# Padding the chunks of split activations and the slots of split weights by 32 bytes, with a smaller descriptor ring

## The chip, the cores and the metric

The kernel runs on one core of a Trainium2 chip. The metric is the device time of one execution in microseconds (us). Each partition of the on-chip memory (SBUF) is a row of bytes; "byte 25184" below means the same place in all 128 partitions.

## The reference

Two transformer blocks run one behind the other on 256 tokens of width 1024, all in float32. The parts that matter here are their matrix products:

```python
def first_block(x, p, ...):
    f = swiglu(rms_norm(h, ffn1_pre_g), ffn1_w_gate, ffn1_w_up, ffn1_w_down)   # 1024 -> 2816 -> 1024
    h = h + 0.5 * rms_norm(f, ffn1_post_g)
    m = hybrid_mixer(rms_norm(h, mix_pre_g), w_in, ..., w_br_attn, w_br_pool, w_out)
    h = h + rms_norm(m, mix_post_g)
    ...                                                                       # a second swiglu
    e = (p @ ple_w_proj) * sigmoid(rms_norm(h, ple_pre_g) @ ple_w_gate)
    return h + rms_norm(e, ple_post_g)

def second_block(x, mem, ...):
    ...                                           # projections, causal attention, a convolution, two gates
    x = x + merged @ w_mix_out
    x = x + memory_cross_attention(rms_norm(x), rms_norm(mem), w_mem_q, w_mem_kv, w_mem_o)
    x = x + (silu(gate) * up) @ w_ffn_out
    return rms_norm(x, norm_final)
```

## The kernel before

All weights come from DRAM as one stream `ws` of 345 units. A unit is 512 KB, eight tiles of 128x128, and lies as 4096 bytes in each partition. SyncE loads units into five `raw` buffers (line 63). ScalarE copies a unit, rounded to the shorter float32r format, into a slot of `wh` (line 90; seven slots), and VectorE writes the rest, `raw - wh`, into a slot of `wl` (line 101; six slots). `Stream.take` hands out the eight tiles of a slot one after another, 512 bytes apart.

Activations are split in the same way. The class `Split` holds them: one tile has chunks of 128 channels, and a chunk is 1024 bytes of high part (256 tokens) and then 1024 bytes of low part. So chunk k begins 2048 k bytes behind chunk 0. `x` (eight chunks), `a` (22 chunks, inside the feed-forward layers), `o`, `y`, `m`, `mo`, `p` and `x2` are such tiles.

A product of a weight tile and a chunk takes the terms high by high, low by high and high by low. There are two forms, and the words below are used from here on:

- a **group of three** (`mm3`): three matmuls of 256 columns, `wh` on x high, `wl` on x high, `wh` on x low.
- a **pair** (`mm2`): one matmul of 512 columns (`wh` on high and low, which lie side by side) and one of 256 columns (`wl` on high). The feed-forward layers use it for most of their work.

In `mm3t` the roles are changed: the activations are the weights of TensorE and four tiles of a `wh` or `wl` slot (512 columns) are streamed past them. It is used for the values in `first_group`, with `x`, and in `mem_v_task`, with `m` and 256 columns.

Every matmul brings a weight load of 128x128 (PEld in the profile) which overlaps the matmul ahead of it. Every matmul is issued from line 197, whichever helper calls it. The order on each engine is the order in which the program is written; nothing is scheduled later.

Where the tiles lie follows from their sizes in the order of their making. `x` begins at byte 25184, `a` at 141536, `m` at 212960, `y` of the first mixer at 187616, the first slot of `wh` at 72512 and of `wl` at 101184. Divided by 128, every split activation leaves 96 and every weight slot 64.

GpSimd issues 36 small DMAs by itself; their descriptors stand in a ring that takes the first 16384 bytes of each partition. Thirteen times it also raises a sum of squares to the power -1/2 (line 286), on which a stage's scaling waits. `load_kv` (line 1118) fetches keys and values of the memory attention with eight of these DMAs.

Of the kernel before, what the change touches and what calls it, by code (L numbers as in the profile page):

```python
# [11 lines left out]
F32R = mybir.dt.float32r  # L12
# [3 lines left out]
P = 128  # L16
T = 256
D = 1024
DC = D // P
FF = 2816  # L20
FC = FF // P
# [5 lines left out]
UB = 8  # L27
LA = 4
RAW_BUFS = 5
HL_BUFS = 6  # L30
NUNITS = 345
WARM = 3
START = {0: (2, 2, 4), 1: (4, 4), 2: (4, 4), 3: (4, 4), 4: (4, 4)}

GAINS = ["ffn1_pre_g", "ffn1_post_g", "mix_pre_g", "mix_post_g", "ffn2_pre_g", "ffn2_post_g",
# [14 lines left out]
class Stream:  # L50
# [20 lines left out]
    def split_now(self, u, cuts=(UB,)):  # L71

        assert self.nhigh == self.nlow == u
        h = self.hl.tile([P, UB * P], F32R, tag="wh", name="wh", bufs=HL_BUFS + 1)
        l = self.hl.tile([P, UB * P], F32R, tag="wl", name="wl")
        r = self.R.pop(u)
        for s in self.parts(cuts):
            self.nc.scalar.copy(out=h[:, s], in_=r[:, s])  # L78
            self.nc.vector.tensor_tensor(out=l[:, s], in0=r[:, s], in1=h[:, s].bitcast(F32), op=ALU.subtract)  # L79
        self.H[u], self.L[u] = h, l  # L80
        self.nhigh = self.nlow = u + 1
# [4 lines left out]
    def split(self, u):  # L86
        while self.nhigh <= min(u + 1, NUNITS - 1):
            self.load(self.nhigh + RAW_BUFS - 2)
            h = self.hl.tile([P, UB * P], F32R, tag="wh", name="wh", bufs=HL_BUFS + 1)
            self.nc.scalar.copy(out=h, in_=self.R[self.nhigh])  # L90
            self.H[self.nhigh] = h
            self.nhigh += 1
            if self.nlow < self.nhigh - 1:
                self.low()
        while self.nlow <= min(u, NUNITS - 1):
            self.low()

    def low(self):
        u = self.nlow
        l = self.hl.tile([P, UB * P], F32R, tag="wl", name="wl")  # L100
        self.nc.vector.tensor_tensor(out=l, in0=self.R.pop(u), in1=self.H[u].bitcast(F32), op=ALU.subtract)  # L101
        self.L[u] = l
        self.nlow += 1
# [23 lines left out]
class Split:  # L127


    def __init__(self, t):  # L130
        self.t = t

    def __getitem__(self, i):
        return self.t[:, :, i]
# [5 lines left out]
class Net:  # L140
# [89 lines left out]
    def setup(self):  # L230
        nc, b, d = self.nc, self.base, self.d
        hg = b.tile([P, G_ALL + DC * T], F32, name="hg")
        self.gv, self.h = hg[:, 0:G_ALL], hg[:, G_ALL:].rearrange("p (c t) -> p c t", c=DC)
        self.x = Split(b.tile([P, DC, 2, T], F32R, name="x"))
        self.fg = b.tile([P, DC, T], F32, name="fg")
        self.ident = b.tile([P, P], F32, name="ident")
        self.ones = b.tile([P, 1], F32, name="ones")
        self.mhalf = b.tile([P, 2], F32, name="mhalf")
        self.half = b.tile([P, 4 * DC], F32, name="half")
        nc.scalar.preload_act_table_set("silu_and_others")  # L240
        at = [(0, 1), (1, 1), (2, 2), (4, 2), (6, 2)]
        for u, (lo, n) in enumerate(at):
            s = slice(G_ALL + lo * T if lo else 0, G_ALL + (lo + n) * T)
            nc.sync.dma_start(out=hg[:, s], in_=d["gx"][:, s])
            self.ws.load(u, START.get(u, (UB,)))
        nc.gpsimd.memset(self.ones, 1.0)
        nc.gpsimd.memset(self.mhalf, -0.5)
        idle = self.fg[:, 0]
        nc.vector.memset(idle, 0.0)
        w = self.abank()  # L250
        for _ in range(WARM):
            nc.tensor.matmul(w.t[:, 0:T], idle[:, 0:P], idle, start=True, stop=True)
        nc.gpsimd.dma_start(out=self.ident, in_=d["cst"][:, C_ID:C_ID + P])
        self.identr = b.tile([P, P], F32R, name="identr")
        self.after(1, lambda: nc.vector.tensor_copy(out=self.identr, in_=self.ident))
# [174 lines left out]
    def ffn(self, gate, up, down, on_chunk, nk=4):  # L430
        nc = self.nc
        x = self.x
        with self.tc.tile_pool(name="ffn", bufs=1, reuse_waits="tile") as fp:
            self.fp = fp
            a = Split(fp.tile([P, FC, 2, T], F32R, name="a"))
            aH, aL = a[0], a[1]

            def zt():
                return fp.tile([P, 2, T], F32, tag="z", name="z", bufs=6)

            def join2(z, b):
                nc.scalar.copy(out=z, in_=b.t[:, 1])  # L442
                nc.vector.tensor_tensor(out=z, in0=b.t[:, 0], in1=z, op=ALU.add)  # L443

            def evac(m, z, src):
                nc.vector.tensor_tensor(out=z, in0=src, in1=self.row(rs), op=ALU.mult)  # L446
                nc.scalar.activation(out=z[:, 0], in_=z[:, 0], func=AF.Silu)  # L447

                def s1():
                    nc.vector.tensor_tensor(out=z[:, 0], in0=z[:, 0], in1=z[:, 1], op=ALU.mult)  # L450

                def s2():
                    nc.scalar.copy(out=aH[:, m], in_=z[:, 0])

                def s3():
                    nc.vector.tensor_tensor(out=aL[:, m], in0=z[:, 0], in1=aH[:, m].bitcast(F32), op=ALU.subtract)

                self.after(1, s1)
                self.after(2, s2)
                self.after(3, s3)  # L460

            bs = [self.bank() for _ in range(nk)]
            for k in range(DC):
                for m in range(nk):
                    for sub, (name, off) in enumerate((gate, up)):
                        w = self.ws.take(name, k, off + m)
                        self.mm3(bs[m], bs[m].t[:, sub], w, x.at(k), stop=k == DC - 1)
                if k == DC - 2:
                    r = self.stat([self.acc])
                self.tick()  # L470
            rs = self.bcast_sb(r)
            for m in range(nk):
                evac(m, zt(), bs[m].t)
            for m in range(nk, FC):
                z = zt()
                for sub, (name, off) in enumerate((gate, up)):
                    b = self.bank()
                    self.wide(b, name, off + m, range(DC), x)
                    join2(z[:, sub], b)
                    if sub == 1:  # L480
                        evac(m, z, z)
                    self.tick()
            for c in range(DC):
                b = self.bank()
                two = c < DC - 1
                for k in range(FC):
                    w = self.ws.take(down, k, c)
                    if two:
                        self.mm2(b, w, a.at(k), stop=k == FC - 1)
                    else:  # L490
                        self.mm3(b, b.t[:, 0], w, a.at(k), stop=k == FC - 1)
                    if k % 8 == 4:
                        self.tick()
                on_chunk(c, b.t[:, 0], b.t[:, 1] if two else None)
# [185 lines left out]
    def mixer1(self, fills):  # L680
        nc, tc, d = self.nc, self.tc, self.d
        with tc.tile_pool(name="mix1", bufs=1, reuse_waits="tile") as mp:
# [6 lines left out]
            cnt = mp.tile([P, 4, 2, 8], F32, name="cnt")  # L689
            nc.gpsimd.dma_start(out=cnt.rearrange("p a e t -> p (a e t)"), in_=d["cst"][:, C_CNT:C_CNT + 64])  # L690
            tg2 = mp.tile([P, 4, 2, T], F32, name="tg2")
            o = Split(mp.tile([P, 4, 2, T], F32R, name="o"))
            y = Split(mp.tile([P, 4, 2, T], F32R, name="y"))
            oH, oL, yH, yL = o[0], o[1], y[0], y[1]
            tg1 = self.fg.rearrange("p (a b) t -> p a b t", b=2)

# [237 lines left out]
    def mixer2(self, x2):  # L934
        nc, tc, d = self.nc, self.tc, self.d
        W = T + P
        with tc.tile_pool(name="mix2", bufs=1, reuse_waits="tile") as mp:
# [2 lines left out]
            vz = mp.tile([P, 2, 4, 2, P], F32, name="vz")  # L940
            cv = mp.tile([P, 4, T], F32, name="cv")
            tg2 = mp.tile([P, 4, 2, T], F32, name="tg2")
            o = Split(mp.tile([P, 4, 2, T], F32R, name="o"))
            y = Split(mp.tile([P, 4, 2, T], F32R, name="y"))
            oH, oL, yH, yL = o[0], o[1], y[0], y[1]
            cs = mp.tile([P, 2, T], F32, tag="ct", name="ct", bufs=3).rearrange("p a t -> p (a t)")[:, 0:3 * P]
            tg1 = self.fg.rearrange("p (a b) t -> p a b t", b=2)
# [154 lines left out]
    def memory(self, x2):  # L1102
        nc, tc, d = self.nc, self.tc, self.d
        with tc.tile_pool(name="mem", bufs=1, reuse_waits="tile") as mp:
# [1 line left out]
            kH, kL = kx[0], kx[1]  # L1106
            vH = mp.tile([P, 2, D], F32R, name="mvH")
            vL = mp.tile([P, 2, D], F32R, name="mvL")
            o = Split(mp.tile([P, DC, 2, T], F32R, name="mo"))
            oH, oL = o[0], o[1]  # L1110

            def split(t, h, l):
# [73 lines left out]

            def trans(h):
                b = self.transposed(st[h])
                p = Split(mp.tile([P, 2, 2, T], F32R, tag="p", name="p", bufs=2))
                pH, pL = p[0], p[1]  # L1190
                bt = b.t.rearrange("p (a t) -> p a t", a=2)
                nc.scalar.copy(out=pH, in_=bt)
# [97 lines left out]
    def run(self):  # L1290
# [11 lines left out]
        self.vd = self.dram.tile([P, 2, D], F32, name="vd")  # L1302
        memctx = ExitStack()
        mpool = memctx.enter_context(tc.tile_pool(name="memx", bufs=1, side="right"))
        self.m = Split(mpool.tile([P, DC, 2, T], F32R, name="m"))
        self.mH, self.mL = self.m[0], self.m[1]
        for c in range(DC):
            self.after(14 + 3 * c, lambda c=c: self.mem_prep_chunk(c))
# [14 lines left out]
        gp2 = self.halved(1, "ffn2_post_g", 0.5)  # L1323
        plectx = ExitStack()
        self.plep = plectx.enter_context(tc.tile_pool(name="plep", bufs=1, side="right"))
        self.p = Split(self.plep.tile([P, 2, 2, T], F32R, name="p"))
        self.pH, self.pL = self.p[0], self.p[1]

        def prep_p():
# [15 lines left out]
        memctx.close()  # L1345
        self.dump("h4")
        with tc.tile_pool(name="x2p", bufs=1, side="right", reuse_waits="tile") as xp2:
            x2 = Split(xp2.tile([P, DC, 2, T], F32R, name="x2"))
            self.mixer2(x2)
            self.dump("h5")  # L1350
            self.memory(x2)
# [100 lines left out]
```

## Time and profile before

| | us |
|---|---|
| median of 2 runs | 1035.32 (1035.19 to 1035.44) |
| profiled execution, device time | 1035.02 |
| its span, first to last instruction | 1032.9 |
| PE busy | 1023.2 |
| DVE busy | 758.4 |
| ACT busy | 585.2 |
| POOL busy | 44.0 |

The device time is 2.1 us longer than the span, for what lies around it. PE is TensorE, DVE VectorE, ACT ScalarE, POOL GpSimd and SP SyncE. Matmuls are pipelined: the duration of one (its column "mean ns") is longer than the step from its start to the start of the next, and it is the steps that add up to the span. The timeline view gives starts to 0.01 us, and joins equal neighbours in one row with their count.

### The profile page before, as it was taken

Reading aid. Unit: us, or ns where it says so; the run is one execution under the profiler, and the core shown is the slowest. Engines: PE = TensorE matmul, PEld = TensorE weight load, DVE = VectorE, ACT = ScalarE, POOL = GpSimd, SP = SyncE. Lnnn points to the kernel's source line nnn. Section 1 sums busy time; section 2 is a strip of 40 time slices with the busy share of each in tenths; the row PEclk is TensorE's granted clock in tenths of the full one; section 3 lists DMA queues with packets and bytes.
Section 4 is the critical chain, followed back from the end, with each engine's and each line's share of the span. In section 5 each row is a group of like instructions: output and inputs, shape, how many; then the busy total and the mean of one; then the engine's idle time right before and its main releaser. Section 6 shows DMA issues by size and latency. Waiting matters only on the chain.

```text
span 1032.9 us, 18212 instructions
## 1 busy us (share of the span) xinstructions
PE 1023.2 (99%) x7280; PEld 961.8 (93%) x7280; DVE 758.4 (73%) x1191; ACT 585.2 (57%) x979; POOL 44.0 (4%) x73
## 2 busy tenths in 40 slices
PE   9999999999999999999999999999999999999997
PEld 8988888999999998888899999999999999888886
DVE  7798865687868678888457776886678767878652
ACT  7567655464644556655456565464556555656531
POOL 0000000120000110000000111000001000000000
PEclk9999999999999999999999999999999999999999
DMA  8676665555545755666645666554566345766541
GB/s 292 221 217 193 204 212 175 194 191 183 195 143 168 230 181 174 194 201 185 204 170 178 201 199 199 156 176 151 163 218 232 106 136 198 216 186 185 183 161 42
DMA packets 55013, 191.34 MB, mean 185 GB/s; under 512 B 6400, under 2 KB 7936, under 8 KB 54928
## 3 DMA queue, kind: packets, MB, share of 16 engines
q1 hardware_dynamic: 52992, 184.37, 55.2%
q0 software_dynamic: 1936, 5.80, 1.9%
q8 instruction: 57, 0.93, 0.4%
q14 instruction: 28, 0.23, 0.1%
HBM read 187.00 MB, written 3.15 MB: 184 GB/s over the span
## 4 chain that ended last, share of the span: by engine, by line
PE 81%; issue 16%; DMA 1%; DVE 1%; SPq 0%; POOL 0%; POOLq 0%; DVEq 0%; ACT 0%
PE mm L197 77%; PE at L197 3%; DMA raw<-ws 1%; PE at L876 1%; DMA hg<-gx 0%; DVE sqp L337 0%; POOL r L286 0%; DVE wl L79 0%; SPq L63 0%; DVE wl L101 0%; DVE x L312 0%; DVE fg L1363 0%; POOLq L1445 0%; DVEq L1445 0%; ACT wh L78 0%
## 5 line engine op out<-in xcount | busy, mean ns | idle before, releaser
L197 PE MATMUL mm<-x,wh 128*128 128x256 f32 (+1 forms) x2784 | 650.3, 315 | 0.1
L197 PE MATMUL mm<-x,wl 128*128 128x256 f32 x1824 | 512.3, 281 | 0.9 <-DVE wl L101 0.4
L197 PEld LDWEIGHTS mm<-x,wh 128*128 128x128 f32 x2784 | 459.5, 188 | 35.5 <-ACT wh L78 1.0
L101 DVE TENSOR_TENSOR wl<-raw,wh 128x1024 fp32r<-128x1024 f32 x340 | 409.1, 1218 | 11.4 <-ACT wh L90 5.2
L90 ACT CAST wh<-raw 128x1024 fp32r<-128x1024 f32 x340 | 349.3, 1046 | 39.5 <-PE mm L197 30.3
L197 PEld LDWEIGHTS mm<-x,wl 128*128 128x128 f32 x1824 | 343.8, 189 | 2.7 <-DVE wl L79 1.2
L197 PE MATMUL mm<-a,wh 128*128 128x512 f32 (+1 forms) x594 | 185.2, 368 | 0.0
L197 PE MATMUL mm<-a,wl 128*128 128x256 f32 x528 | 147.5, 280 | 0.0
L197 PEld LDWEIGHTS mm<-a,wh 128*128 128x128 f32 x594 | 107.2, 188 | 19.1
L197 PEld LDWEIGHTS mm<-a,wl 128*128 128x128 f32 x528 | 99.2, 188 | 0.0
L447 ACT ACTIVATE z<-z 128x256 f32<-128x256 f32 x66 | 27.2, 418 | 80.5 <-DVE z L446 80.5
L443 DVE TENSOR_TENSOR z<-mm,z 128x256 f32<-128x256 f32 x108 | 45.3, 420 | 30.0 <-ACT z L442 29.8
L442 ACT COPY z<-mm 128x256 f32<-128x256 f32 x108 | 39.5, 366 | 33.0 <-PE mm L197 32.7
L308 ACT ACTIVATE x<-hg 128x256 fp32r<-128x256 f32 x56 | 27.5, 537 | 42.3 <-DVE hg L381 22.1
L286 POOL TENSOR_TENSOR r<-v,mhalf 128x2 f32<-128x2 f32 x13 | 17.6, 1354 | 677.6 <-DVE v L284 677.6
L446 DVE TENSOR_TENSOR z<-z,rs 128x512 f32<-128x512 f32 x54 | 37.4, 692 | 1.8
L353 DVE TENSOR_TENSOR fg<-mm,fg 128x256 f32<-128x256 f32 x14 | 5.9, 425 | 40.7 <-ACT fg L352 40.7
L450 DVE TENSOR_TENSOR z<-z 128x256 f32<-128x256 f32 x66 | 27.2, 424 | 8.1 <-ACT z L447 2.7
L312 DVE SCALAR_TENSOR_TENSOR x<-hg,x 128x256 fp32r<-128x256 f32 x56 | 26.8, 514 | 6.8 <-ACT x L308 6.8
L352 ACT COPY fg<-mm 128x256 f32<-128x256 f32 x14 | 5.2, 373 | 42.0 <-PE mm L197 42.0
L327 DVE TENSOR_TENSOR acc<-acc,sq 128x256 f32<-128x256 f32 x27 | 11.5, 425 | 23.6 <-ACT sq L326 23.5
L197 PE MATMUL mm<-y,wh 128*128 128x256 f32 x136 | 27.8, 283 | 0.0
(217 smaller groups left out, 1033.6 us busy)
## 6 DMA issues: line engine op xcount, KB each, us to landing
raw<-ws SPq DMA_DIRECT2D x340, 512.0 KB, 4.1
raw<-ws SPq DMA_DIRECT2D x9, 256.0 KB, 5.8
ub<-ub SPq DMA_DIRECT2D x8, 160.0 KB, 2.8
mraw<-memT POOLq DMA_DIRECT2D x8, 128.0 KB, 4.2
kd<-kv POOLq DMA_DIRECT2D x8, 128.0 KB, 3.3
vd<-kv POOLq DMA_DIRECT2D x4, 256.0 KB, 4.3
kv<-kd POOLq DMA_DIRECT2D x4, 256.0 KB, 5.9
kv<-vd POOLq DMA_DIRECT2D x4, 256.0 KB, 6.7
```

The lines of the kernel that those rows point to most:

```text
L90: self.nc.scalar.copy(out=h, in_=self.R[self.nhigh])
L101: self.nc.vector.tensor_tensor(out=l, in0=self.R.pop(u), in1=self.H[u].bitcast(F32), op=ALU.subtract)
L197: self.nc.tensor.matmul(out, lhsT, rhs, start=not b.started, stop=stop, skip_group_check=True)
L286: nc.gpsimd.tensor_tensor(out=r, in0=v, in1=self.mhalf, op=ALU.pow)
L308: self.nc.scalar.activation(out=self.ordered(x[0][:, c]), in_=self.rows(self.h[:, c]), func=AF.Copy, scale=gain(c))
L312: self.nc.vector.scalar_tensor_tensor(out=l, in0=self.rows(self.h[:, c]), scalar=gain(c), in1=h, op0=ALU.mult, op1=ALU.subtract)
L327: nc.vector.tensor_tensor(out=acc, in0=acc, in1=s, op=ALU.add)
L442: nc.scalar.copy(out=z, in_=b.t[:, 1])
L443: nc.vector.tensor_tensor(out=z, in0=b.t[:, 0], in1=z, op=ALU.add)
L446: nc.vector.tensor_tensor(out=z, in0=src, in1=self.row(rs), op=ALU.mult)
L447: nc.scalar.activation(out=z[:, 0], in_=z[:, 0], func=AF.Silu)
L450: nc.vector.tensor_tensor(out=z[:, 0], in0=z[:, 0], in1=z[:, 1], op=ALU.mult)
```

## The change

Each chunk of a split activation gets 8 more float32 (32 bytes) behind its low part, so that chunk k begins 2080 k bytes behind chunk 0. Each slot of `wh` and `wl` gets 32 bytes as well, so that slots lie 4128 bytes apart; the tiles inside a slot stay 512 bytes apart. `raw` is not changed. GpSimd's ring is cut from 16384 to 8192 bytes in each partition, and the room takes the padding. No instruction is added, removed, moved or given another shape; the order on every engine is the same.

After it, `x` begins at byte 16992, `a` at 134016, the first slot of `wh` at 64576 and of `wl` at 93472. Divided by 128, the chunks of an activation leave 96, 0, 32, 64, 96 and so on for k = 0, 1, 2, 3, 4 (for `a` and those behind it the row begins at another place), and the slots of `wh` leave 64, 96, 0, 32 and so on.

```diff
+SKEW = 8
...
+    def high(self):
+        return self.hl.tile([P, UB * P + SKEW], F32R, tag="wh", name="wh", bufs=HL_BUFS + 1)[:, 0:UB * P]
+
+    def low_tile(self):
+        return self.hl.tile([P, UB * P + SKEW], F32R, tag="wl", name="wl")[:, 0:UB * P]
...
     def __init__(self, t):
-        self.t = t
+        self.t = t[:, :, 0:2 * T].rearrange("p n (i t) -> p n i t", i=2)
...
-        self.x = Split(b.tile([P, DC, 2, T], F32R, name="x"))
+        self.x = Split(b.tile([P, DC, 2 * T + SKEW], F32R, name="x"))
...
-            a = Split(fp.tile([P, FC, 2, T], F32R, name="a"))
+            a = Split(fp.tile([P, FC, 2 * T + SKEW], F32R, name="a"))
...
-    nc = bacc.Bacc("TRN2", target_bir_lowering=False, num_devices=1)
+    nc = bacc.Bacc("TRN2", target_bir_lowering=False, num_devices=1, dynamic_dma_scratch_size=8192)
```

The tiles `o`, `y`, `mo`, `p`, `m` and `x2` are changed as `x` and `a` are.

## Rows read from the trace of the kernel before

**Rows 1.** The page: span, busy time of each engine, granted clock.

```profile
span 1032.9 us, 18212 instructions
...
PE 1023.2 (99%) x7280; PEld 961.8 (93%) x7280; DVE 758.4 (73%) x1191; ACT 585.2 (57%) x979; POOL 44.0 (4%) x73
...
PEclk9999999999999999999999999999999999999999
```

**Rows 2.** Groups of instructions of PE, each shape apart.

```profile
L197 PE MATMUL mm<-x,wl 128*128 128x256 f32 x1824 | 512.3, 281 | 0.9 <-DVE wl L101 0.4 <-DVE wl L79 0.4
L197 PE MATMUL mm<-x,wh 128*128 128x256 f32 x1920 | 350.1, 281 | 0.1
L197 PE MATMUL mm<-x,wh 128*128 128x512 f32 x864 | 300.2, 391 | 0.0
L197 PE MATMUL mm<-a,wh 128*128 128x512 f32 x462 | 161.1, 393 | 0.0
```

**Rows 3.** The chain that ended last, in order of time: start us, us, what.

```profile
30.37 83.22 PE mm L197 x480
```

**Rows 4.** Timeline of PE, first feed-forward layer: pairs (start us, us).

```profile
60.03 0.39 PE L197 MATMUL mm<-x,wh 128*128 128x512 f32 x1
60.26 0.28 PE L197 MATMUL mm<-x,wl 128*128 128x256 f32 x1
60.38 0.39 PE L197 MATMUL mm<-x,wh 128*128 128x512 f32 x1
```

**Rows 5.** Timeline of PE, merge of the first mixer: groups of three.

```profile
314.90 0.28 PE L197 MATMUL mm<-y,wl 128*128 128x256 f32 x1
...
315.26 0.28 PE L197 MATMUL mm<-y,wl 128*128 128x256 f32 x1
...
315.62 0.28 PE L197 MATMUL mm<-y,wl 128*128 128x256 f32 x1
```

**Rows 6.** Timeline of PE, output product of the first mixer; three groups between these rows.

```profile
339.79 0.28 PE L197 MATMUL mm<-x,wl 128*128 128x256 f32 x1
...
341.19 0.28 PE L197 MATMUL mm<-x,wl 128*128 128x256 f32 x1
```

**Rows 7.** Timeline of PE, the same product of the second mixer, as many groups.

```profile
764.84 0.28 PE L197 MATMUL mm<-x,wl 128*128 128x256 f32 x1
...
766.25 0.28 PE L197 MATMUL mm<-x,wl 128*128 128x256 f32 x1
```

**Rows 8.** Timeline of PE, `mem_v_task`: weight slots streamed past `m`, as many groups.

```profile
590.80 0.28 PE L197 MATMUL mm<-wl,m 128*128 128x256 f32 x1
...
592.24 0.28 PE L197 MATMUL mm<-wl,m 128*128 128x256 f32 x1
```

**Rows 9.** Timeline of PE, `first_group` of the second mixer: six matmuls of 512 columns.

```profile
612.92 0.39 PE L197 MATMUL mm<-wh,x 128*128 128x512 f32 x1
613.15 0.40 PE L197 MATMUL mm<-wl,x 128*128 128x512 f32 x1
613.38 0.63 PE L197 MATMUL mm<-wh,x 128*128 128x512 f32 x2
...
614.32 0.28 PE L197 MATMUL mm<-x,wh 128*128 128x256 f32 x1
```

**Rows 10.** DMA view of 750 to 800 us: busy tenths in 40 slices.

```profile
DMA  7557167988999960573814838039019999689997
```

**Rows 11.** Timeline of POOL, the loads of `load_kv` and the power between them.

```profile
756.70 1.12 POOL L1118 DMA_DIRECT2D kv<-kd  x2 [101.11 <-PE mm L197]
757.81 0.73 POOL L1118 DMA_DIRECT2D kv<-vd  x1
758.53 0.56 POOL L1118 DMA_DIRECT2D kv<-kd  x1
...
789.61 1.11 POOL L286 TENSOR_TENSOR r<-v,mhalf 128x2 f32<-128x2 f32 x1 [1.01 <-DVE v L284]
```

**Rows 12.** Line 1118 in the trace: time from issue to landing.

```profile
DMA to landing us min/median/max: 5.1/6.2/7.8
```

More of the change, by code (lines that the diff above doesn't have):

```diff
@@ L73, in split_now @@
         assert self.nhigh == self.nlow == u
-        h = self.hl.tile([P, UB * P], F32R, tag="wh", name="wh", bufs=HL_BUFS + 1)
-        l = self.hl.tile([P, UB * P], F32R, tag="wl", name="wl")
+        h, l = self.high(), self.low_tile()
         r = self.R.pop(u)
@@ L88, in split @@
             self.load(self.nhigh + RAW_BUFS - 2)
-            h = self.hl.tile([P, UB * P], F32R, tag="wh", name="wh", bufs=HL_BUFS + 1)
+            h = self.high()
             self.nc.scalar.copy(out=h, in_=self.R[self.nhigh])
@@ L96, in split @@
             self.low()
+    def high(self):
+        return self.hl.tile([P, UB * P + SKEW], F32R, tag="wh", name="wh", bufs=HL_BUFS + 1)[:, 0:UB * P]
+    def low_tile(self):
+        return self.hl.tile([P, UB * P + SKEW], F32R, tag="wl", name="wl")[:, 0:UB * P]
     def low(self):
         u = self.nlow
-        l = self.hl.tile([P, UB * P], F32R, tag="wl", name="wl")
+        l = self.low_tile()
         self.nc.vector.tensor_tensor(out=l, in0=self.R.pop(u), in1=self.H[u].bitcast(F32), op=ALU.subtract)
@@ L691, in mixer1 @@
             tg2 = mp.tile([P, 4, 2, T], F32, name="tg2")
-            o = Split(mp.tile([P, 4, 2, T], F32R, name="o"))
-            y = Split(mp.tile([P, 4, 2, T], F32R, name="y"))
+            o = Split(mp.tile([P, 4, 2 * T + SKEW], F32R, name="o"))
+            y = Split(mp.tile([P, 4, 2 * T + SKEW], F32R, name="y"))
             oH, oL, yH, yL = o[0], o[1], y[0], y[1]
@@ L942, in mixer2 @@
             tg2 = mp.tile([P, 4, 2, T], F32, name="tg2")
-            o = Split(mp.tile([P, 4, 2, T], F32R, name="o"))
-            y = Split(mp.tile([P, 4, 2, T], F32R, name="y"))
+            o = Split(mp.tile([P, 4, 2 * T + SKEW], F32R, name="o"))
+            y = Split(mp.tile([P, 4, 2 * T + SKEW], F32R, name="y"))
             oH, oL, yH, yL = o[0], o[1], y[0], y[1]
@@ L1108, in memory @@
             vL = mp.tile([P, 2, D], F32R, name="mvL")
-            o = Split(mp.tile([P, DC, 2, T], F32R, name="mo"))
+            o = Split(mp.tile([P, DC, 2 * T + SKEW], F32R, name="mo"))
             oH, oL = o[0], o[1]
@@ L1188, in trans @@
                 b = self.transposed(st[h])
-                p = Split(mp.tile([P, 2, 2, T], F32R, tag="p", name="p", bufs=2))
+                p = Split(mp.tile([P, 2, 2 * T + SKEW], F32R, tag="p", name="p", bufs=2))
                 pH, pL = p[0], p[1]
@@ L1304, in run @@
         mpool = memctx.enter_context(tc.tile_pool(name="memx", bufs=1, side="right"))
-        self.m = Split(mpool.tile([P, DC, 2, T], F32R, name="m"))
+        self.m = Split(mpool.tile([P, DC, 2 * T + SKEW], F32R, name="m"))
         self.mH, self.mL = self.m[0], self.m[1]
@@ L1325, in run @@
         self.plep = plectx.enter_context(tc.tile_pool(name="plep", bufs=1, side="right"))
-        self.p = Split(self.plep.tile([P, 2, 2, T], F32R, name="p"))
+        self.p = Split(self.plep.tile([P, 2, 2 * T + SKEW], F32R, name="p"))
         self.pH, self.pL = self.p[0], self.p[1]
@@ L1347, in run @@
         with tc.tile_pool(name="x2p", bufs=1, side="right", reuse_waits="tile") as xp2:
-            x2 = Split(xp2.tile([P, DC, 2, T], F32R, name="x2"))
+            x2 = Split(xp2.tile([P, DC, 2 * T + SKEW], F32R, name="x2"))
             self.mixer2(x2)
```

## The prediction

> **What bounds the kernel now.** I read the page first. [...] So nothing that ends a wait earlier can help much: about 10 us of the span are not PE's. A change pays, or costs, through the step from one matmul to the next.
>
> The groups by shape [rows 2] say how much there is of what. There are 864 + 462 = 1326 matmuls of 512 columns on `x` and `a`, so 1326 pairs. Of 7280 matmuls that leaves 7280 - 2 x 1326 = 4628, nearly all of 256 columns in groups of three, so about 1500 groups.
>
> The chain and the timeline give the steps, since durations of pipelined matmuls overlap. The chain has a stretch of 480 matmuls, 240 pairs, in 83.22 us [rows 3]: 346.7 ns a pair. Inside a pair the 512 columns take 0.23 us and the 256 columns 0.12 [rows 4]; the mean over the 240 pairs of that stretch, of starts that the view rounds, is 228.3 and 118.3 ns. So a pair takes 0.3467 us and 1326 of them 460 us. The remaining 573 us are mostly groups of three. These do not all cost the same: 0.36 us in the first mixer's merge [rows 5]; (341.19 - 339.79) / 4 = 0.350 in its output product [rows 6]; 1.41 / 4 = 0.3525 in the second mixer's output product [rows 7].
>
> Two things in this matter here. First, the 256 columns that a matmul of 512 has more than one of 256 take 228.3 - 118.3 = 110 ns. A matmul of 256 columns takes 116.7 (0.350 / 3) to 120, so some 7 to 10 ns of each step are not streaming; in a pair it is 8.3. This is all that any placement of data could give back. Second, [rows 6] and [rows 7] are the same code on the same tile `x` with the same tiles inside slots, and differ by 2.5 ns a group, 0.7%, with no change of place at all.
>
> **The change part by part.** No instruction is added, taken away or reshaped, so there is no work to count. What changes is where a streamed chunk lies against the weight tile that is loaded under it. That is a price per matmul, times some 7000.
>
> Does the place matter? Before, the remainders by 128 of all streamed activations (96) and all weight slots (64) are fixed, so their distance is always 32. Beyond this, distances by 512 differ between tiles: 288 for `x`, 416 for `a`, `y` and `o`. Pairs on `x` and on `a` show no difference that I can find in their groups (mean duration 391 and 393 ns) [rows 2]. For the groups of three, tiles at 416 take 0.36 us [rows 5] and the tile at 288 takes 0.350 or 0.3525 [rows 6, 7]. That could be the place, or the rhythm in which PE happens to run: the 2.5 ns between rows 6 and 7 are rhythm alone.
>
> The other distances stand in the trace where the roles are changed. With a slot streamed past `m` (distance 96 by 128) the four groups take 1.44 us, 0.360 each [rows 8]. With a slot streamed past `x` (96 as well) six matmuls of 512 columns take 614.32 - 612.92 = 1.40 us, 233.3 ns each [rows 9], where a pair's 512 columns take 228.3 (346.7 less 118.3, the 256 columns). So what there is of another distance is 5 ns dearer per 512 columns, and at the dear end for 256. This speaks for a small loss, not for a gain; but these rows have another operand in each role, so it is no proof.
>
> The row on the first cause that comes to mind, other traffic, is against it: between 757 and 777 us the DMA engines go from idle to full and back [rows 10] and the groups keep their 0.3525 us [rows 7]. So the lost 8.3 ns lie between PE's own two streams or inside PE.
>
> [...]
>
> For the sum I take this: pairs stay at 346.7 ns, since both tiles that use them have that step. Groups of three lose today's rhythm, because distances now change from chunk to chunk, and get a mean of the three steps seen, (350 + 352.5 + 360) / 3 = 354.2 ns. Today's mean I estimate at 351.5, as 1920 / 2 = 960 of the 1500 groups are on `x` [rows 2]. So 1500 x 2.7 ns = 4.0 us more. The bounds lie 8.3 ns a matmul below (7000 x 8.3 = 58 us) and, above, at the dearest steps seen: per pair 233.3 - 228.3 = 5.0 and 120 - 118.3 = 1.7, so 1326 x 6.7 = 8.9 us, and per group 360 - 351.5 = 8.5, so 1500 x 8.5 = 12.8 us; together 21.7 us.
>
> The other engines are bystanders. DVE and ACT read and write the padded tiles along the partition as before; they are busy 73% and 57% of the span [rows 1], and a per cent on their instructions would stay under PE. If that cover were gone, PE would wait for `wl`, which it now does for 0.9 us in all [rows 2].
>
> The ring: GpSimd issues four loads in 756.70 to 759.09, of 256 KB each, with no gap between them [rows 11], while each takes 5.1 to 7.8 us to land [rows 12]. So four were in flight in 16 KB of ring. If half the ring held only two, the third would wait up to 6 us; behind it on POOL's queue stand the fourth load and, 31 us later, the power at 789.61. Both have that slack, so I cost it at nothing.
>
> Against its own time the profiled execution becomes 1035.0 + 4.0 = 1039.0; it is 0.3 us under the median of 1035.3, which makes 1039.3. I forecast 1039.
>
> **The rivals.** *Other distances are dearer (slower).* One mechanism: PE's weight load and its stream disturb each other, least at the distance of 32 that all tiles now have. After the change three quarters of the matmuls have another one. Price: 0.75 x 21.7 = 16 us, 1051; if the quarter that stands nowhere in the trace (64) is worse than these, more. It passes 2% (20.7 us) from 3.0 ns a matmul on the mean of 7000. For it: [rows 8, 9]. Against it: the changed roles, and that `a` and `x` agree.
>
> *The padding breaks a collision (faster).* The 8.3 ns are then a collision that comes of everything being a power of two apart, and distances that move from chunk to chunk avoid it in half of the cases: 0.5 x 58 = 29 us, 1006. For it: the loss is the same on nearly every matmul, as a fixed alignment would make it. Against it: the distances 288, 416 (by 512) and those of [rows 8, 9] all have it. [...]
>
> *The ring bites.* POOL's loads wait for ring space one by one, and the power that scales the queries comes late. Price: at most about 8 us, the longest landing, so 1043. Against it: the 31 us between these loads and the power [rows 11].
>
> **How the numbers follow.** Forecast (no price beyond rhythm, 1031 to 1045): 0.55. Dearer distances: 0.28, about half of it beyond 2%. Collision broken: 0.14, most of it beyond 2%. Ring: 0.03. So faster by over 2% (under 1014.6; about what a measurement of this kernel can tell from no change) 0.12, slower by over 2% (above 1056) 0.15, and the rest, 0.73, within. The range reaches from the collision rival's middle (1008) to somewhat over the dear rows (1058).
>
> **What the profile will show.** If I am right, pairs on `x` step by 346 to 348 ns and groups of three by 350 to 357, with the DVE and ACT rows unchanged. Pairs above 350 mean the dearer distances; pairs under 340 mean the collision. A step that changes with chunk k inside one product would show that distance itself has the price. I am wrong if 64, the distance that no row shows, is far from the others, or if the remainder of the streamed chunk counts by itself: 0 and 32 by 128 are new as well.

## The result, and the profile after

The changed kernel takes 1042.71 us (1042.06 to 1043.36, 2 runs), 1.0074 of the kernel before, interval 1.0057 to 1.0091. So it is slower by 7.4 us, inside the range on record and 3.7 us above the forecast of 1039.0. The profiled execution took 1042.06 us for a span of 1039.9.

The page of the changed kernel, as in [rows 1]:

```profile
span 1039.9 us, 18204 instructions
...
PE 1030.8 (99%) x7280; PEld 964.5 (93%) x7280; DVE 758.3 (73%) x1191; ACT 584.9 (56%) x979; POOL 44.0 (4%) x73
...
PEclk9999999999999999999999999999999999999999
```

PE does the same 7280 matmuls at the same granted clock (a mean of 0.998 of full speed in both) and is busy 7.6 us longer; DVE, ACT and POOL did not move. The count of 18204 instructions is short of [rows 1] by 8 semaphore waits of PE, which are no work; with the small ring alone it is 18204 as well (a_ring below). The groups of PE by shape (busy us, mean ns), as in [rows 2], the matmul line now being L203:

```profile
L203 PE MATMUL mm<-x,wl 128*128 128x256 f32 x1824 | 512.0, 281 | 0.2 <-DVE wl L79 0.2
L203 PE MATMUL mm<-x,wh 128*128 128x256 f32 x1920 | 354.2, 282 | 0.1
L203 PE MATMUL mm<-x,wh 128*128 128x512 f32 x864 | 303.4, 395 | 0.0
L203 PE MATMUL mm<-a,wh 128*128 128x512 f32 x462 | 162.8, 396 | 0.0
```

The matmuls of 512 columns became longer (391 to 395 and 393 to 396 ns), and nothing waits more. The chain of the changed kernel (start us, us, what, matmuls) has these two pieces; the first is cut at the same places as [rows 3]:

```profile
29.86 84.13 PE mm L203 x480
...
307.99 46.81 PE mm L203 x396
```

480 matmuls are 240 pairs: 84.13 us, 350.5 ns a pair, where [rows 3] had 346.7. The 396 are 132 groups of three of the first mixer's merge and output product: 354.6 ns each. In the chain of the kernel before these took 355.2:

```profile
305.95 46.88 PE mm L197 x396
```

The timeline in the first feed-forward layer, as in [rows 4]:

```profile
60.24 0.39 PE L203 MATMUL mm<-x,wh 128*128 128x512 f32 x1
60.47 0.28 PE L203 MATMUL mm<-x,wl 128*128 128x256 f32 x1
60.58 0.39 PE L203 MATMUL mm<-x,wh 128*128 128x512 f32 x1
60.81 0.28 PE L203 MATMUL mm<-x,wl 128*128 128x256 f32 x1
60.93 0.40 PE L203 MATMUL mm<-x,wh 128*128 128x512 f32 x1
61.16 0.28 PE L203 MATMUL mm<-x,wl 128*128 128x256 f32 x1
61.29 0.39 PE L203 MATMUL mm<-x,wh 128*128 128x512 f32 x1
```

The lines show three pairs of 0.34, 0.35 and 0.36 us: the even beat of [rows 4] is gone, and the step changes from one pair to the next.

Where the time went, from the starts of the same matmuls in both traces:

| stretch | before us | after us | difference |
|---|---|---|---|
| three feed-forward layers without their first groups (1326 pairs and a few groups) | 488.44 | 493.39 | +4.95 |
| first groups of layers 2 and 3 | 46.47 | 47.02 | +0.55 |
| first mixer | 151.55 | 152.32 | +0.77 |
| second mixer | 191.88 | 193.11 | +1.23 |
| ple, joins, memory | 114.54 | 114.61 | +0.07 |
| start, up to the pairs | 26.03 | 25.58 | -0.45 |

They add up to 7.1 us of the span's 7.0. By form, and from the start of the pairs on, the same starts give +4.83 us for the 1326 pairs, 3.6 ns each, +3.3 us for the 1238 groups of three, and -0.6 us for all other matmuls. Where one group follows another without a wait, the mean step of a group went from 351.8 to 354.7 ns.

POOL's loads in the changed kernel, as in [rows 11] and [rows 12]:

```profile
761.84 1.12 POOL L1124 DMA_DIRECT2D kv<-kd  x2 [101.99 <-PE mm L203]
762.95 0.73 POOL L1124 DMA_DIRECT2D kv<-vd  x1
763.67 0.57 POOL L1124 DMA_DIRECT2D kv<-kd  x1
...
DMA to landing us min/median/max: 4.3/6.9/8.0
```

Four loads still go out one behind the other, and land in 4.3 to 8.0 us where it was 5.1 to 7.8.

### The profile page after: what moved, and what is told of

It reads as the page before. It is cut to its first block, busy times and chain, and to the rows that moved or that the text cites. A ratio compares the mean times of both kernels' runs of the same rounds, so it can differ in the third digit from the quotient of the medians.

```text
span 1039.9 us, 18204 instructions
## 1 busy us (share of the span) xinstructions
PE 1030.8 (99%) x7280; PEld 964.5 (93%) x7280; DVE 758.3 (73%) x1191; ACT 584.9 (56%) x979; POOL 44.0 (4%) x73
## 4 chain that ended last, share of the span: by engine, by line
PE 82%; issue 16%; DMA 0%; POOL 0%; DVE 0%; SPq 0%; POOLq 0%; DVEq 0%; ACT 0%
PE mm L203 79%; PE at L203 3%; PE at L882 1%; DMA raw<-ws 0%; POOL r L292 0%; SPq L64 0%; DVE fg L1369 0%; POOLq L1451 0%; DVE wl L79 0%; DVEq L1451 0%; ACT wh L78 0%; SPq L250 0%; DVE v L290 0%
## 5 line engine op out<-in xcount | busy, mean ns | idle before, releaser
L203 PE MATMUL mm<-x,wh 128*128 128x256 f32 (+1 forms) x2784 | 657.6, 317 | 0.1
L203 PE MATMUL mm<-x,wl 128*128 128x256 f32 x1824 | 512.0, 281 | 0.2 <-DVE wl L79 0.2
L203 PEld LDWEIGHTS mm<-x,wh 128*128 128x128 f32 x2784 | 461.2, 188 | 39.8 <-ACT wh L78 0.9
L107 DVE TENSOR_TENSOR wl<-raw,wh 128x1024 fp32r<-128x1024 f32 x340 | 409.0, 1218 | 12.3 <-ACT wh L90 6.2
L203 PEld LDWEIGHTS mm<-x,wl 128*128 128x128 f32 x1824 | 343.7, 188 | 1.6 <-DVE wl L79 0.9
L203 PE MATMUL mm<-a,wh 128*128 128x512 f32 (+1 forms) x594 | 186.9, 370 | 0.0
L203 PE MATMUL mm<-a,wl 128*128 128x256 f32 x528 | 147.8, 280 | 0.0
L203 PEld LDWEIGHTS mm<-a,wh 128*128 128x128 f32 x594 | 107.3, 188 | 20.3
L203 PEld LDWEIGHTS mm<-a,wl 128*128 128x128 f32 x528 | 99.5, 188 | 0.0
L203 PE MATMUL mm<-y,wh 128*128 128x256 f32 x136 | 27.6, 282 | 0.0
```

The costliest lines, as they stand in the source:

```text
L203: self.nc.tensor.matmul(out, lhsT, rhs, start=not b.started, stop=stop, skip_group_check=True)
```

## The experiments

In all of them, "distance" is the place of the streamed chunk less that of the weight tile loaded under it, and "by 128" or "by 512" is the remainder of it. "Constant" means that it stays the same from matmul to matmul; it "turns" where chunks or slots are no longer a multiple of 512 apart. All kernels but the one before have the 8 KB ring. The 240 pairs and the 132 groups are the two stretches of the chain named above; a mean over a stretch hides how single steps differ, and at the distance of 32 the 355.2 ns are 360 in the merge and 350 in the output product. Each ratio is to runs of the kernel before that were taken beside it (medians 1035.1 to 1035.3 us).

| kernel | distance by 128 | 240 pairs, us (ns each) | 132 groups, us (ns each) | time us | ratio to before, interval |
|---|---|---|---|---|---|
| before | 32 constant | 83.22 (346.7) | 46.88 (355.2) | 1035.32 | |
| after | all four, turning | 84.13 (350.5) | 46.81 (354.6) | 1042.71 | 1.0074 [1.0057, 1.0091] |
| a_ring | 32 constant | 83.22 (346.7) | 46.88 (355.2) | 1035.08 | 1.0001 [0.9992, 1.0010] |
| b_chunks | all four, turning with the chunk | 84.20 (350.8) | 46.77 (354.3) | 1042.54 | 1.0072 [1.0057, 1.0087] |
| c_slots | all four, turning with the slot | 83.88 (349.5) | 46.70 (353.8) | 1041.48 | 1.0061 [1.0044, 1.0078] |
| d_128 | 32, turning by 512 | 83.81 (349.2) | 46.73 (354.0) | 1041.09 | 1.0057 [1.0042, 1.0072] |
| e_d64 | 64 constant | 84.78 (353.3) | 44.95 (340.5) | 1035.33 | 1.0001 [0.9991, 1.0010] |
| f_d0 | 0 constant | 83.21 (346.7) | 47.50 (359.8) | 1045.32 | 1.0099 [1.0084, 1.0114] |
| g_d96 | 96 constant | 84.79 (353.3) | 46.87 (355.1) | 1047.56 | 1.0120 [1.0103, 1.0137] |
| i_512 | 32 constant | 83.22 (346.7) | 46.88 (355.2) | 1035.11 | 1.0001 [0.9992, 1.0010] |
| l_256 | 32 constant, other by 512 | 83.22 (346.7) | 46.88 (355.2) | 1035.03 | 0.9998 [0.9989, 1.0007] |
| j_views | pairs 32, groups 64, constant | 83.21 (346.7) | 44.95 (340.5) | 1027.53 | 0.9924 [0.9909, 0.9939] |
| k_three | 64 constant, groups only | | 44.95 (340.5) | 1032.67 | 0.9972 [0.9963, 0.9982] |
| m_48 | pairs 48 and 16, groups 64 | 84.00 (350.0) | 44.94 (340.5) | 1031.28 | 0.9960 [0.9946, 0.9975] |

**The parts of the change.** The theory to begin with was the prediction's rival, that distances by 128 other than 32 are dear; against it stood that the ring or the padded slots alone cost the time.

a_ring, the ring alone:

```diff
-    nc = bacc.Bacc("TRN2", target_bir_lowering=False, num_devices=1)
+    nc = bacc.Bacc("TRN2", target_bir_lowering=False, num_devices=1, dynamic_dma_scratch_size=8192)
```

> Only the ring is cut to 8192 bytes; no padding, so every tile lies 8 KB lower and all distances by 128 are 32 as before. Both theories of the padding, and the theory that the ring costs nothing: pairs step by 346.7 ns, 1035 us (1034 to 1037). If the ring bites: above 1038, with the load_kv rows of POOL later or longer.

The ring is free (1035.08 us, 1.0001 of before), and so is the shift of all tiles by 8192 bytes that comes with it. The pieces of its chain that are compared here and below agree with those of before to 0.01 us:

```profile
30.02 83.22 PE mm L204 x480
119.68 73.65 PE mm L204 x450
...
305.58 46.88 PE mm L204 x396
...
383.80 162.40 PE mm L204 x962
```

From here on SKEW is the padding of a chunk and SLOT that of a slot, in numbers of 4 bytes. b_chunks pads the chunks alone:

```diff
+SKEW = 8
+SLOT = 0
...
+        self.x = Split(b.tile([P, DC, 2 * T + SKEW], F32R, name="x"))
```

> Only the chunks are padded by 32 bytes; slots lie 4096 bytes apart. The distance by 128 then moves by 32 with every weight tile taken (k runs innermost in the feed-forward layers). Theory of the change (a distance that changes from matmul to matmul breaks PE's even step): pairs at about 350 ns as with the whole change, 1040 to 1044 us. Rival (some distances are dear whatever came before, 96 above all): a quarter of the pairs at each distance, mean 350 as well, but those at 32 back at 346.7.

c_slots pads the slots alone:

```diff
+SKEW = 0
+SLOT = 8
...
+        return self.hl.tile([P, UB * P + SLOT], F32R, tag="wl", name="wl")[:, 0:UB * P]
```

> Only the slots are padded by 32 bytes; chunks lie 2048 bytes apart. Inside a slot the eight weight tiles keep one distance; wh and wl have different ones, so a pair's two matmuls alternate between two distances, and both change at each new slot. Theory of the change of distance: between nothing and the whole, 1037 to 1042 us, the lost time behind slot changes or where wh and wl differ. Rival of the dear distance: slots at distance 96 cost 3 to 6 ns a pair more for all of their eight tiles, the others nothing, 1037 to 1039 us.

Either padding alone costs nearly all of it, +7.4 and +6.3 us, and the two together no more than one. In b_chunks the step of a matmul of 512 columns on `x` goes with its distance by 512, which takes eight values as k runs from 0 to 7: from 229.1 ns at 224 to 235.9 at 192, each with a spread under 1 ns over the three layers (starts of the trace, sorted by the addresses of the tiles). So the step does depend on the place. The rival expected here, a price for each distance by 128, falls: pairs at 32 by 128 take 350.8 ns with k = 0 and 346.7 with k = 4, pairs at 96 take 353.9 with k = 2 and 346.7 with k = 6. What was not separated in this run is the distance and what went ahead of it, since the chunks always come in the same order. c_slots lies in the range of the first theory, above that of its rival.

d_128 pads both by 128 bytes, so that the distance by 128 stays 32:

```diff
+SKEW = 32
+SLOT = 32
```

> Chunks and slots are padded by 128 bytes in place of 32, so strides are no power of two and no multiple of 512, but all distances by 128 stay 32. Theory that only the remainder by 128 counts: pairs at 346.7 ns, 1035 us (1034 to 1037). Rival (a stride that is a multiple of 512 or 2048 is what keeps the step even, or distances by 256 and 512 count): 1040 us or more, as with the whole change.

The theory that only the remainder by 128 counts falls: 1041.1 us though it never changes. The chain of d_128:

```profile
30.27 83.81 PE mm L204 x480
...
307.66 46.73 PE mm L204 x396
```

**Constant distances.** The next theory was that any constant distance is as good as today's, and that what costs is the turning alone. Here strides are those of the kernel before, and a spare tile ahead of the weight buffers and one behind them shift the weights:

```diff
+            ep(tc.tile_pool(name="padw", bufs=1)).tile([P, PAD_W], F32, name="padw")
...
+            ep(tc.tile_pool(name="pada", bufs=1)).tile([P, PAD_A], F32, name="pada")
```

PAD_W and PAD_A are 24 and 8 in e_d64, 8 and 24 in f_d0, 16 and 16 in g_d96, 64 and 64 in l_256.

> Chunks, slots and order as in the kernel before; a tile of 96 bytes ahead of the weight buffers and one of 32 behind them shift only the distance between a matmul's two operands: 64 by 128 bytes for every matmul where it was 32, and constant. By 512 it is 192 on x, 448 on a, 64 on m. Theory (what costs is that the position by 512 changes from one matmul to the next; a constant distance of any size is as good as today's): pairs 346.7 ns, groups of three 351 to 353, the time 1034 to 1037 us. Rival (each distance by 512 has its own price, as the run with padded chunks showed them: 235.9 ns for 512 columns at 192, 233.2 at 64): pairs on x 351 to 355 ns, the time 1040 to 1046 us.

> As the run before it with the two tiles exchanged, 32 bytes ahead of the weight buffers and 96 behind them: the distance by 128 bytes is 0 everywhere, by 512 it is 256 on x, 0 on a and 128 on m. Theory (a constant distance of any size is as good as today's): pairs 346.7 ns, 1034 to 1037 us. Rival (each distance by 512 has its price; 256 had 232.4 ns for 512 columns): pairs on x about 351 ns, 1038 to 1043 us. If operands that start in one place by 128 bytes collide, it is the worst of the three: over 1045 us.

> 64 bytes ahead of the weight buffers and 64 behind them: the distance by 128 bytes is 96 everywhere, by 512 it is 224 on x, 480 on a and 96 on m. Theory (constant distance is as good as today's): pairs 346.7 ns, 1034 to 1037 us. Rival (prices by distance): 224 was the cheapest on x in the run with padded chunks, 229.1 ns for 512 columns, so pairs about 348 ns, 1036 to 1039 us on that stage's count; by the prediction's own rival that 96 by 128 is dear, 1045 us or more.

Chain of e_d64, pairs and groups:

```profile
30.15 84.78 PE mm L210 x480
...
308.14 44.95 PE mm L210 x396
```

Chain of f_d0:

```profile
30.36 83.21 PE mm L210 x480
120.02 75.06 PE mm L210 x450
...
309.19 47.50 PE mm L210 x396
...
388.63 162.56 PE mm L210 x962
```

Chain of g_d96:

```profile
31.18 84.79 PE mm L210 x480
...
310.66 46.87 PE mm L210 x396
```

Half of that theory falls: a constant distance has a price, and it is another one for pairs than for groups of three. By form, as in the result above and against a_ring: e_d64 pays 8.7 us for its pairs and wins 7.7 on its groups of three, f_d0 pays 1.5 and 8.9, g_d96 8.7 and 4.3. So the median of e_d64 equals before by accident: its pairs lose 6.6 ns each, and its groups in the 46.88 us win 14.7. The rival does not hold either, as distances priced by b_chunks misjudge these: 224 was the cheapest there and is as dear as any in g_d96. Of the further expectations, g_d96 came out as the prediction's rival has it (over 1045 us), and f_d0 is over 1045 us too, but by its groups and not as the worst of the three. In f_d0 the pairs on `a` are part of the piece of 450 matmuls: 75.06 us where a_ring has 73.65, while the second layer, in the piece of 962, takes 162.56 where it has 162.40. The same distance on the same code thus cost 1.4 us in one layer and 0.2 in another.

Nor does a constant distance mean an even beat. The starts of g_d96 in the first feed-forward layer:

```profile
62.10 0.40 PE L210 MATMUL mm<-x,wh 128*128 128x512 f32 x1
62.34 0.28 PE L210 MATMUL mm<-x,wl 128*128 128x256 f32 x1
62.47 0.39 PE L210 MATMUL mm<-x,wh 128*128 128x512 f32 x1
62.69 0.28 PE L210 MATMUL mm<-x,wl 128*128 128x256 f32 x1
62.81 0.40 PE L210 MATMUL mm<-x,wh 128*128 128x512 f32 x1
```

Its pairs take 0.37 and 0.34 us in turn; over the 240 pairs the two values are 360.7 and 345.9 ns, and 353.3 is their mean. In f_d0 they are 350.0 and 343.4, and 346.7 is the mean. At 32 and at 64 nearly all pairs take the one value of the table.

i_512 pads the slots by 512 bytes, so that no slot stride is a power of two and every place by 512 stays:

```diff
+SKEW = 0
+SLOT = 128
```

> Slots of wh and wl padded by 512 bytes (4608 apart), chunks as before: no slot stride is a power of two any more, but every position by 512 is as in the kernel before. Theory (positions by 512 count, and their staying constant): pairs 346.7 ns, merge of the first mixer as before, the time 1034 to 1037 us. Rival (the power-of-two stride itself is what kept the rhythm, any padding breaks it): pairs 349 to 351 ns, 1039 to 1043 us.

1035.1: it is not the power-of-two stride of the slots that matters. This and l_256 bear out what is left of the theory:

> Strides as in the kernel before, weights shifted by 256 bytes against the activations: the distance by 128 bytes stays 32, by 512 it is 32 on x and 160 on a where before it was 288 and 416, and constant. In the run with both paddings of 128 bytes all four occurred in turn and it took 1041.1 us. Theory (only the remainder by 128 has a price where it is constant, and the turns by 512 cost by themselves): pairs 346.7 ns, 1034 to 1037 us. Rival (32 and 160 by 512 are dear in themselves, and the run with 128 bytes of padding is the mean of good and bad ones): pairs 351 to 357 ns, 1042 to 1048 us.

l_256 has the distances by 512 (32 on `x`, 160 on `a`) that d_128 added to those of before, and costs nothing:

```profile
30.93 83.22 PE mm L210 x480
...
306.47 46.88 PE mm L210 x396
```

So both sets of distances are free where they are constant (1035.03 us here and 1035.08 in a_ring), 32 and 288 as they were run on `x`, 160 and 416 on `a`. In d_128, which goes through all four at an unchanged distance by 128, 5.9 us are the price of the turning. No run turned chunks and slots together so that the distance stays; whether it is the distance that must stay or the place of each operand by 512 is open.

**Each form at its own distance.** j_views gives the pairs 32 and the groups of three 64, with two views of one `x` tile, 96 bytes apart; each stage takes its own:

```diff
+        xt = b.tile([P, DC * 2 * T + 24], F32R, name="x")
+        self.x3, self.x2 = (Split(xt[:, i:i + DC * 2 * T].rearrange("p (n c) -> p n c", n=DC)) for i in (0, 24))
...
+            fp.tile([P, 120], F32, name="padx")
...
+        self.x = self.x3
         self.join(gain("mix_pre_g"), (4, 8, 12))
...
+        self.x = self.x2
         self.join(gain("ffn2_pre_g"), (4, 8, 12))
```

> Strides as in the kernel before and weights as in the run with distance 64; the x tile is 96 bytes longer and has two views, 96 bytes apart: the stages that work in groups of three use the one at distance 64, the feed-forward layers the one at distance 32, and a begins 480 bytes later, at distance 32 too. Theory now (each constant distance by 128 has a price of its own for each form: pairs 346.7 ns at 32, 353.2 at 64; groups of three 351.6 at 32, 344.7 at 64): pairs back at 346.7, mixers, merges and out products as in the run with distance 64, together 8.7 us less than there, so 1025 to 1029 us, faster than both kernels. Rival (the differences belong to whole programs, or to how all tiles lie, not to the distance in a stage): the stages don't fall apart like this, and the time stays at 1033 to 1037 us.

1027.53 us, 7.7 us faster than the kernel before and 15.2 faster than the changed one, as expected. The pairs of before and the groups of e_d64 stand beside each other in its chain:

```profile
30.16 83.21 PE mm L210 x480
...
305.41 44.95 PE mm L210 x396
```

Its weight slots lie where those of e_d64 lie, and moving the pairs' `x` by 96 bytes gave them their 346.7 ns back; from a_ring to e_d64 `x` stayed, and moving the weights took these away. So it is the place of the two operands to each other that counts, not that of one.

k_three issues every pair as a group of three at distance 64:

```diff
-        self.mm(b, b.t, w[0], x[2])
-        self.mm(b, b.t[:, 0], w[1], x[0], stop=stop)
+        self.mm(b, b.t[:, 0], w[0], x[0])
+        self.mm(b, b.t[:, 0], w[1], x[0])
+        self.mm(b, b.t[:, 1], w[0], x[1], stop=stop)
```

> As the run with distance 64, and every pair is issued as three matmuls of 256 columns (wh on high, wl on high into the first half of the bank, wh on low into the second), 1326 matmuls more, same sums. Theory (it is the form that decides what distance 64 costs: a matmul of 512 columns takes 235 ns there, two of 256 columns about 229.5): 344.7 ns in place of 353.9 for each, 12 us less than there: 1021 to 1026 us. Rival (what makes the feed-forward stages slow at 64 is the place of their tiles or their traffic, not the 512 columns): 353 to 360 ns each, 1035 to 1044 us.

1032.67 is between the two expectations. Its chain tells why:

```profile
30.35 84.80 PE mm L210 x720
121.70 72.15 PE mm L210 x636
...
305.61 44.95 PE mm L210 x396
...
381.98 165.36 PE mm L210 x1404
```

720 matmuls are 240 groups, 353.3 ns each; 636 are 212 groups, 340.3; 1404 are 468 groups, 353.3. It is the same form at the same distance in the same program. At 64 nearly every group takes either 340 or 353.3 ns and stays with it over a whole product, often a whole stage; e_d64 has both as well, in products of eight groups that follow one another, and the 344.7 that the expectation was built on was a mean of the two. What decides between them is open.

m_48 puts the pairs' view of `x` at 48 and `a` at 16 (the line for `x`, against j_views):

```diff
-        self.x3, self.x2 = (Split(xt[:, i:i + DC * 2 * T].rearrange("p (n c) -> p n c", n=DC)) for i in (0, 24))
+        self.x3, self.x2 = (Split(xt[:, i:i + DC * 2 * T].rearrange("p (n c) -> p n c", n=DC)) for i in (8, 4))
```

> The kernel with two views of x again, with the view of the feed-forward layers at distance 48 and a at distance 16 by 128 bytes, where both were at 32; groups of three stay at 64 (those on m go to 32, as in the kernel before, under 1 us). Pairs took 346.7 ns at the distances 0 and 32, and 353.2 at 64 and 96. Theory (the price of a pair depends on which half of the 128 bytes the distance lies in): 346.7 ns at 48 and at 16, the time 1026 to 1029 us. Rival (places off the grid of 32 bytes cost, or the price is finer): pairs above 350 ns, 1031 us or more; and if 48 or 16 were better than 32, below 1024 us, which neither expects.

1031.28, so the theory of halves falls. Pairs on `x` at 48 take 84.00 / 240 = 350.0 ns, neither 346.7 nor 353.3; by the starts they take 353.0 and 347.0 in turn:

```profile
31.31 84.00 PE mm L210 x480
121.80 73.82 PE mm L210 x450
```

The second piece, mostly pairs on `a` at 16, stays within 0.2 us of the 73.65 at 32. So the grid of 32 bytes is not a condition by itself, and 48 is dearer for pairs than 32.

## Why the prediction was nearly right

**What bounds the kernel**: right. By the two pages 9.7 us of the span of before are not PE's and 9.1 of the changed one's (1039.9 less 1030.8). All of the change came through PE's steps; the waits of its groups, 0.9 us and less in [rows 2], did not grow.

**The failed step** is "pairs stay at 346.7 ns, since both tiles that use them have that step". That two tiles at distances 288 and 416 agree was read as "the place does not matter for pairs". Both are 32 by 128, and both are constant: the trace of before had no pair whose distance turns. The turning by 512 alone costs a pair 2.5 ns (d_128 against a_ring), and 2.8 to 4.1 where the distance by 128 turns too (c_slots, after, b_chunks). The term put at 0 measured +4.83 us, more than all of the groups. By the signs set down with the forecast, pairs of 350.5 ns stood for its rival of dearer distances; only the groups, at 354.6, kept to its own.

**The groups of three**: sign and price were right, the count was too high. +4.0 us were forecast and 3.3 measured. The step went from 351.8 to 354.7 ns where 351.5 to 354.2 was forecast, but the program has 1302 groups and not 1500: 7280 also counts products with the roles changed, transposes and the attention. The price was partly luck, as the two means were not formed alike (today's leant on the 960 groups on `x`, the new one counted three steps as equals), and not all groups moved one way: those at 360 in [rows 5] became faster. In the first mixer the merge went from 23.15 to 22.85 us, while its tasks went from 80.95 to 81.77. That 1039 came near 1042.7 is luck in the same measure: most of the loss came from the form that was put at nothing.

**The rhythm**, which the forecast saw behind the groups alone, is there for both forms. The step of [rows 7] is 353.3 ns over the whole product (the 0.3525 came of rounded starts), that of [rows 6] 350.0: like k_three's, two beats of the same code at the same distance. With constant distances most long stretches settle at a mean of 340.0 (groups, merge of e_d64), 346.7 (pairs, a_ring), 350.0 ([rows 6]), 353.3 ([rows 7]) or 360.0 ns ([rows 5]), all whole multiples of 3.33 ns; on `x` in f_d0, g_d96 and m_48 it is only the mean of two neighbouring pairs that does. The groups of g_d96 settle on none (351 to 359 ns), and with turning distances pairs run at means of 349 to 351.

**The rival of dearer distances** had the right cause in part. Constant 96 costs 12.3 us and constant 0 10.1. But "least at the distance of 32" is wrong for groups of three: 64, the distance that no row showed, is the best one for them, and far from the others, which the prediction had named as a sign of being wrong. The mean of the four constant kernels, (1035.1 + 1035.3 + 1045.3 + 1047.6) / 4 = 1040.8, is close to the changed kernel's 1042.7. That proves little, since d_128 pays 5.9 us without ever leaving 32. How the 7.4 us divide between dearer distances and turning was not separated. The price of 16 us took the dearest rows for all; [rows 9], 233.3 ns for 512 columns with the roles changed, was a fair guess for pairs (228.3 became about 232.7 in the mean).

**The collision that the padding breaks**: not by this change. But the wish behind it, that the lost 7 to 10 ns of a step can be had back, came true in part in j_views, by choosing one distance and not by varying it. At 340.5 ns a group takes 113.5 ns a matmul, where [rows 6] and [rows 5] have 116.7 and 120; so 3.5 ns are left above the 110 ns that the prediction, by its estimate from the steps, gives to 256 columns.

**PE's own streams, not other traffic**: borne out as far as the runs go. With the instructions and their order unchanged, the places of PE's two operands alone moved the time from 1027.5 us (j_views) to 1047.6 (g_d96). Whether the two wait on each other at SBUF or inside PE no run shows. That DMA traffic is not the cause the trace bears out: [rows 7] covers 1.4 us only, but of the 62 groups that begin between 756 and 778 us of the kernel before, 61 step by 353 or 354 ns, with the queues busy and idle [rows 10].

**The other engines and the ring**: both right, 758.3 and 584.9 us busy on DVE and ACT, and a_ring at 1.0001.

## What to carry to other kernels

Where PE is busy 99% of the time and each matmul has its own weight load, the place of the streamed tile against the weight tile can be worth a per cent (0.8% here): try a few constant offsets between the two buffers, apart for each form of matmul, before padding strides, and keep strides at multiples of 512 bytes, as paddings of 32 bytes cost 6.3 to 7.4 us here and those of 128 bytes 5.9, and one of 512 (i_512, the slots alone) cost nothing. Equal medians don't mean that nothing moved, so compare the stretches of the chain one by one: that is how e_d64, 1.0001 of before, led to the fastest kernel.

## What was not expected of the hardware

- A step of PE depends on the distance of its two operands in SBUF: in the same stretches, and in the mean, a pair takes 346.7 ns at 0 and 32 by 128 and 353.3 at 64 and 96, and groups of three take 340.5 at 64, 355 at 32 and 96, and 359.8 at 0. Single steps may alternate at a constant distance: pairs at 96 take 360.7 and 345.9 ns in turn. Which part of the chip makes it so was not seen; no view shows PE's reads.
- Distances that turn cost by themselves: 5.9 us (d_128), though each of them is free when it is constant (a_ring 1035.08 us, l_256 1035.03).
- One and the same code at one distance can run in two beats, 340.3 or 353.3 ns a group, for a whole stage (k_three), and 350.0 or 353.3 in the kernel before ([rows 6] and [rows 7]).
- Half the descriptor ring costs nothing here (a_ring, 1.0001 of before, interval 0.9992 to 1.0010).
